# The identity and the causal mask of forgetting attention, from bfloat16 to float32r

## The chip, the cores and the metric

One core of one Trainium2 chip. The metric is the device time of one execution in microseconds (us). Shorter is better.

## The reference, cut to what matters

A decoder trunk of two layers over 256 tokens of width 1024. Layer 0 mixes tokens with forgetting attention (16 heads of 64), layer 1 with chunkwise retention; each is followed by a mixture of 32 SwiGLU experts of which every token takes two. The change lies in the scores of the attention:

```
def query_block(i):
    ...
    s = jnp.einsum('bhqd,bhkd->bhqk', q_b, k).astype(F32) * scale
    s = s + c_b[..., :, None] - cum[..., None, :]
    q_pos = start + jnp.arange(Q_BLOCK)
    s = jnp.where(k_pos[None, :] <= q_pos[:, None], s, NEG_INF)
    p = jax.nn.softmax(s, axis=-1)
    return jnp.einsum('bhqk,bhkd->bhqd', p.astype(v.dtype), v)
```

with Q_BLOCK = 128 and NEG_INF = -1e30. So of 256 keys, queries 0 to 127 see the keys 0 to 127 under a triangular mask, and queries 128 to 255 see the keys 0 to 127 fully and 128 to 255 under the same triangular mask.

## The kernel before

The program runs through four phases in this order: attention (`phase_a`), the experts of layer 0 (`phase_moe`), retention (`phase_c`), the experts of layer 1. All weights, some 460 MB, are streamed from HBM once, through 26 slots of SBUF of 8 KB per partition each. The queue of SP issues every weight transfer (L169) in a fixed order, each as soon as a slot for it is free; a slot comes free when the last instruction that reads it is done. What paces the stream is therefore the DMA engines where slots are free, and the engines that use up the slots where they are not.

In `phase_a` the projections run as steps, one step per block of 128 input channels. A weight block is cut into a high and a low float32r part by ScalarE (L456) and VectorE (L467), up to four blocks ahead, and TensorE makes three kinds of products from the parts (L500 with 256 moving columns, L512 to L514 with 512). A small list, `steps`, says which other work is put between two steps: `steps.at(n, f)` emits f behind step n. Every engine runs its own instructions in the order of the program.

The heads are worked in eight pairs, at steps 25, 29, 33, 38, 46, 49, 52 and 55. `scores` (L713 to L727) fills two PSUM banks, one for each head of a pair: four terms for the queries 128 to 255 against all 256 keys (L721, 256 columns), four for the queries 0 to 127 against the keys 0 to 127 (L724, 128 columns). These use 64 of the 128 rows of the array, one head the upper and one the lower half. Then the mask is added by products of an identity with a triangle of 0 and -1e30 (L726, L727), all 128 rows, 128 columns, two for each bank and so four for each pair, 32 in all. Identity and triangle, `idb` and `cab`, are bfloat16 views of the tile `half`, which comes by one DMA from a table (L600). In the next steps follow the row maximum (L734, L735), the exponential (L741, L742), the division, three transposes for each head (L765) and the products with the values (L778, L779).

`og` is a slot of eight chunks of 256 float32 columns. Chunks 0 to 3 take the output of the first heads, chunk 4 the running sum of the gate's logarithm, chunk 6 and a part of 7 small weights early on. Chunk 5 is first written by `evict_T` behind step 57, which is behind the last scores.

Of the kernel before, what the change touches and what calls it, by code (L numbers as in the profile page):

```python
# [13 lines left out]
F32R = mybir.dt.float32r  # L14
BF16 = mybir.dt.bfloat16
I32 = mybir.dt.int32
AF = mybir.ActivationFunctionType
# [4 lines left out]
P = 128  # L22
# [208 lines left out]
def trunk(ctx, tc, x, fox_w_in, fox_b_f, fox_w_out, ret_w_in, ret_gn_gain, ret_w_out,  # L231
# [3 lines left out]
    mm = nc.tensor.matmul  # L235
    V, A, G, PE = nc.vector, nc.scalar, nc.gpsimd, nc.tensor
# [5 lines left out]
    def bank(tag, dtype=F32):  # L242
        bufs = {"acc": 4, "sc": 2, "pt": 1, "o": 1}[tag]
        return ps.tile([P, 512], dtype, name=tag, tag=tag, bufs=bufs)

    def small(name, n, bufs=1, dtype=F32):
        return cp.tile([P, n], dtype, name=name, tag=name, bufs=bufs)
# [5 lines left out]
    def new_slot(i, dtype, units=1):  # L253

        k = i, units, dtype
        if k not in made:
            made[k] = nc.alloc_sbuf_tensor_at(f"slot_{len(made)}", [P, 2048 * units], dtype,
                                              offset=slot_base + 8192 * i)
        return made[k].ap()
# [70 lines left out]
    ident = small("ident", P)  # L330
# [41 lines left out]
    idb, cab, trb = (half.bitcast(BF16)[:, P * i:P * i + P] for i in range(3))  # L372
# [202 lines left out]
    def phase_a():  # L575
# [11 lines left out]
        ids = {}  # L587

        def chunks(n, dtype=F32):
            ids[n], a = st.claim(dtype)  # L590
            return a.rearrange("p (c q) -> p c q", c=8)


        og = chunks("og")
        cT, wf = og[:, 4, :], og[:, 6, 0:P].rearrange("p (k h) -> p k h", k=8)
        bf = small("bf", 16)
        for n in range(2):
            nc.sync.dma_start(wf[:, 4 * n:4 * n + 4, :], fw[n][:, :, 4096:4112])
# [35 lines left out]
        steps = Steps()  # L634
# [6 lines left out]
        def forget_0():  # L641
            G.tensor_tensor(wf, wf, gT[:, 0, :, None].to_broadcast([P, 8, 16]), ALU.mult)
            wfb = wf[:, :, None, :].to_broadcast([P, 8, 8, 16])
            G.tensor_copy(wfh.rearrange("p k (r h) -> p k r h", r=8), wfb)

        def forget_half():
            pk = small("pk", 16)
            V.tensor_tensor(pk, bf, cst[:, C_E16:C_E16 + 16], ALU.mult)
            V.tensor_reduce(bfp, pk, AX.X, ALU.add)
            G.tensor_tensor(wf, wf, wfh[:, :, 0:16].bitcast(F32), ALU.subtract)  # L650
            A.activation(wfl.rearrange("p k (r h) -> p k r h", r=8), wf[:, :, None, :].to_broadcast([P, 8, 8, 16]),
                         AF.Copy)
# [60 lines left out]
        def scores(hp):  # L713
            bs = [bank("sc"), bank("sc")]
            pr[hp] = bs
            (qh, ql), (kh, kl) = q2[hp // 4], k2[hp // 4]
            c = hp % 4
            terms = ((ql[:, c], kh[:, c]), (qh[:, c], kh[:, c]), (qh[:, c], kl[:, c]), (bq, bias[:, hp % 7]))
            for i, (q, k) in enumerate(terms):
                for b, r in zip(bs, own):  # L720
                    mm(b[:, 128:384], q[r, 128:256], k[r, :], start=i == 0, stop=False, skip_group_check=True)  # L721
            for q, k in terms:
                for b, r in zip(bs, own):
                    mm(b[:, 0:128], q[r, 0:128], k[r, 0:128], start=False, stop=False, skip_group_check=True)  # L724
            for b in bs:
                mm(b[:, 0:128], idb, cab, start=False, stop=True, skip_group_check=True)  # L726
                mm(b[:, 256:384], idb, cab, start=False, stop=True, skip_group_check=True)  # L727

        nms = {}

# [51 lines left out]
        def heads(hp, s):  # L782
            steps.at(s, lambda: scores(hp))
            steps.at(s + 1, lambda: after_scores(hp))
            steps.at(s + 2, lambda: after_first(hp))
            steps.at(s + 3, lambda: norm(hp, 1))
            steps.at(s + 4, lambda: ptrans(hp, 0))
            steps.at(s + 6, lambda: ptrans(hp, 1))
            steps.at(s + 7, lambda: pv(hp))
# [63 lines left out]
        steps.at(5, row_rstd)  # L853
        steps.at(10, rows)
        steps.at(1, forget_0)
        steps.at(6, forget_half)
        for n, f in ((12, forget_1), (14, forget_2), (17, forget_3), (19, forget_4), (20, forget_5)):
            steps.at(n, f)
        steps.at(30, lambda: router_gains(0, raw))
# [12 lines left out]
        for u in range(2):  # L872
            b = [bank("acc"), bank("acc")]
# [9 lines left out]
            b = [bank("acc"), bank("acc")]  # L883
            proj_T(f"Ak{u}", xs, cuts, b, steps)
            evict_qk(u, b, 1, (17, 41)[u], 1.0)
            b = [bank("acc"), bank("acc")]
            proj_tok(f"Av{u}", xk, cuts, b, steps)
            evict_v(u, b)
        for u in range(2):
            b = [bank("acc"), bank("acc")]  # L890
# [647 lines left out]
    def final_norm():  # L1538
# [34 lines left out]
        yield  # L1573

    g = phase_a()
    if STOP == "A":
        done = True
# [35 lines left out]
```

## Time and profile before

| | us |
|---|---|
| median of 3 runs | 1239.19 |
| lowest and highest run | 1238.94 and 1240.21 |
| the profiled execution | 1238.94 |
| its span, from the first to the last instruction | 1237.0 |
| busy: TensorE matmul | 984.1 |
| busy: TensorE weight load (overlaps the matmuls) | 634.2 |
| busy: VectorE | 413.4 |
| busy: ScalarE | 318.5 |

In the profile PE is TensorE's matmuls, PEld its weight loads, DVE VectorE, ACT ScalarE, SP the engine whose queue issues the weight transfers. A row of the timeline gives start, duration, engine, line, operation and operands, and xN says that N instructions of the same kind in a row are merged into it; with a narrow window the merge is cut to those that overlap the window. Matmuls are pipelined, so their durations overlap; the distance from start to start is what one costs in a stream.

### The profile page before, as it was taken

The page shows a single profiled execution, that of the slowest core. Times are in us where ns is not written, and L with a number is a line of the kernel's source. Part 1 is how long each engine was busy: PE and PEld are TensorE (multiplying, and loading weights), DVE is VectorE, ACT ScalarE, POOL GpSimd, SP SyncE. Part 2 cuts the span into 40 slices and gives each one's busy share as a digit, 9 for nine tenths or more (in the row PEclk, how much of TensorE's full clock was granted, in tenths as well). Part 3 has the DMA queues.
Part 4 walks back from the last instruction along what each step waited for, and adds up shares of the span by engine and source line. Part 5 has one row for each costly group of instructions (what it writes and reads, how often), then busy time and mean ns, then how long its engine had stood idle before and what let it go on. Part 6 is the DMA issues. An engine that isn't in the chain of part 4 may idle for free. (4 is left out here: it accounts for less than half of the span.)

```text
span 1237.0 us, 21654 instructions
## 1 busy us (share of the span) xinstructions
PE 984.1 (80%) x9275; PEld 634.2 (51%) x9275; DVE 413.4 (33%) x934; ACT 318.5 (26%) x674; POOL 38.1 (3%) x46
## 2 busy tenths in 40 slices
PE   9999996686776766678999999987677666667776
PEld 8888863343332323244889888744333333233343
DVE  5776732112111111111678676421211111111112
ACT  5665621011010100000555575321110101100102
POOL 1000000000000000000133100000000000000000
PEclk9999999899987979789999999999999787878899
DMA  9965889999999999999992777989999999999996
GB/s 336 338 260 196 322 303 422 419 426 428 425 427 429 427 426 427 426 429 399 371 369 69 251 259 284 362 363 419 423 427 426 428 428 426 429 425 427 428 424 241
DMA packets 74407, 462.18 MB, mean 374 GB/s; under 512 B 8881, under 2 KB 13761, under 8 KB 42050
## 3 DMA queue, kind: packets, MB, share of 16 engines
q1 hardware_dynamic: 73600, 460.14, 91.8%
q8 instruction: 75, 1.23, 0.4%
q10 hardware_dynamic: 706, 0.60, 0.1%
q14 instruction: 26, 0.21, 0.0%
HBM read 459.67 MB, written 1.05 MB: 372 GB/s over the span
## 5 line engine op out<-in xcount | busy, mean ns | idle before, releaser
L1073 PE MATMUL sc<-slot,slot 128*32 128x256 f32 x4096 | 272.2, 417 | 47.5 <-DMA slot<-in_expert_w_gu_dram 42.9
L1073 PEld LDWEIGHTS sc<-slot,slot 128*32 128x32 f32 x4096 | 136.3, 118 | 171.2 <-issue 54.6
L1104 PE MATMUL o<-slot,half 128*32 128x256 f32 x1984 | 137.3, 421 | 97.7 <-DMA slot<-in_expert_w_down_dram 50.0
L1104 PEld LDWEIGHTS o<-slot,half 128*32 128x32 f32 x1984 | 69.6, 118 | 160.3 <-issue 64.1
L1083 DVE TENSOR_TENSOR rB<-rB,sc 128x128 f32<-128x128 f32 x64 | 23.8, 372 | 373.8 <-ACT rB L1082 373.8
L467 DVE SCALAR_TENSOR_TENSOR slot<-slot,gT,slot 128x512 fp32r<-128x512 f32 x160 | 121.8, 781 | 53.0 <-ACT slot L456 51.6
L500 PE MATMUL acc<-slot,slot 128*128 128x256 f32 x960 | 125.6, 288 | 1.7 <-ACT slot L456 1.3
L456 ACT ACTIVATE slot<-slot,gT 128x512 fp32r<-128x512 f32 x159 | 110.9, 719 | 41.1 <-PE acc L514 15.9
L500 PEld LDWEIGHTS acc<-slot,slot 128*128 128x128 f32 x960 | 119.1, 193 | 4.1 <-ACT slot L456 1.7
L1122 DVE COPY slot<-o 32x256 f32<-32x256 f32 x124 | 51.8, 418 | 197.8 <-PE o L1104 170.5
L1120 ACT ACTIVATE slot<-o 32x256 f32<-32x256 f32 x124 | 46.5, 375 | 276.5 <-DVE slot L1122 276.5
L1082 ACT ACTIVATE rB<-sc 128x128 f32<-128x128 f32 x64 | 17.7, 277 | 360.5 <-PE sc L1073 360.5
L512 PE MATMUL acc<-slot,slot 128*128 128x512 f32 x256 | 102.6, 401 | 0.0
L970 PE MATMUL sc<-h,slot 128*128 128x512 f32 x112 | 75.3, 836 | 33.5 <-DVE slot L957 33.5
L513 PE MATMUL acc<-slot,slot 128*128 128x512 f32 x256 | 100.2, 391 | 1.6 <-DVE slot L467 1.6
L514 PE MATMUL acc<-slot,slot 128*128 128x512 f32 x256 | 100.2, 392 | 0.0
L1133 PE MATMUL acc<-slot,slot 128*128 128x512 f32 (+1 forms) x128 | 60.9, 611 | 13.4 <-ACT slot L1120 13.2
L970 PEld LDWEIGHTS sc<-h,slot 128*128 128x128 f32 x112 | 28.8, 269 | 77.3 <-issue 77.3
L513 PEld LDWEIGHTS acc<-slot,slot 128*128 128x128 f32 x256 | 48.3, 189 | 11.4 <-DVE slot L467 2.5
L514 PEld LDWEIGHTS acc<-slot,slot 128*128 128x128 f32 x256 | 48.1, 188 | 10.1
L512 PEld LDWEIGHTS acc<-slot,slot 128*128 128x128 f32 x256 | 48.2, 188 | 9.3 <-issue 0.3
L978 DVE TENSOR_TENSOR slot<-pt,gT 128x512 f32<-128x512 f32 x28 | 19.4, 692 | 99.1 <-PE pt L977 99.1
(243 smaller groups left out, 756.8 us busy)
## 6 DMA issues: line engine op xcount, KB each, us to landing
slot<-in_expert_w_gu_dram SPq DMA_DIRECT2D x84, 2048.0 KB, 39.1
slot<-in_expert_w_gu_dram SPq DMA_DIRECT2D x86, 1024.0 KB, 9.5
slot<-in_expert_w_down_dram SPq DMA_DIRECT2D x42, 2048.0 KB, 39.1
slot<-in_expert_w_down_dram SPq DMA_DIRECT2D x40, 1024.0 KB, 10.7
slot<-in_ret_w_in_dram SPq DMA_DIRECT2D x24, 1024.0 KB, 14.1
slot<-in_fox_w_in_dram SPq DMA_DIRECT2D x15, 1024.0 KB, 11.8
slot<-in_ret_w_out_dram SPq DMA_DIRECT2D x8, 1024.0 KB, 8.2
slot<-in_fox_w_out_dram SPq DMA_DIRECT2D x4, 1024.0 KB, 15.2
```

The source lines that it names most:

```text
L456: A.activation(wh, w, AF.Copy, scale=1.0 if g is None else g)
L467: V.scalar_tensor_tensor(wl, w, g, wh, ALU.mult, ALU.subtract)
L500: mm(o, w[:, P * j:P * j + P], x[:, k, :], start=first and k == 0 and j % 2 == 0, stop=last and k == 7, skip_group_check=True)
L512: mm(banks[t], xh[:, q], wh, start=first and k == ks[0], stop=False)
L513: mm(banks[t], xh[:, q], wl, start=False, stop=False)
L514: mm(banks[t], xl[:, q], wh, start=False, stop=last and k == ks[-1])
L970: mm(b, o[:, t, :], h[:, t, 512 * n:512 * n + 512], start=t == 0, stop=t == 1)
L1073: mm(bgu[32 * j:32 * j + 32, 0:256].rearrange("p (two f) -> p two f", two=2), xg[:, kk, 32 * e4:32 * e4 + 32], wv[:, :, P * j:P * j + P], ...
L1104: mm(by[32 * nb:32 * nb + 32, 0:256], gTt[:, 32 * j:32 * j + 32], w[:, j % n, 256 * nb:256 * nb + 256], start=j == 0, stop=j == 3, skip_gr ...
L1120: A.activation(o, i, AF.Copy)
L1122: V.tensor_copy(o, i)
L1133: mm(sums[t, n], w2["scm"][0:rows, P * t:P * t + P], y4[0:rows, 512 * n:512 * n + 512], start=start, stop=False, skip_group_check=True)
```

## The change

A float32r view of chunk 5 of the slot `og` takes a copy of the identity and of the triangle. Two new ScalarE instructions, put behind step 11, make these copies from the bfloat16 views. The 32 mask products read the copies in place of the bfloat16 views.

```
+        idca = new_slot(ids["og"], F32R).rearrange("p (c q) -> p c q", c=8)[:, 5, :]
+        idr, car = idca[:, 0:P], idca[:, P:]
...
+        def masks():
+            A.activation(idr, ident, AF.Copy)
+            A.activation(car, cab, AF.Copy)
...
             for b in bs:
-                mm(b[:, 0:128], idb, cab, start=False, stop=True, skip_group_check=True)
-                mm(b[:, 256:384], idb, cab, start=False, stop=True, skip_group_check=True)
+                mm(b[:, 0:128], idr, car, start=False, stop=True, skip_group_check=True)
+                mm(b[:, 256:384], idr, car, start=False, stop=True, skip_group_check=True)
...
         steps.at(6, forget_half)
+        steps.at(11, masks)
```

The identity is copied from the float32 tile `ident`, the triangle from `cab`.

## Rows read from the trace of the kernel before

**Rows 1.** The page's second part: the span in 40 slices of 31 us, busy tenths of TensorE, and the mean busy share of the DMA engines.
```profile
PE   9999996686776766678999999987677666667776
...
DMA  9965889999999999999992777989999999999996
```
**Rows 2.** The chain of work that ended last, in order of time: start, duration, what. Its pieces before 918 us are TensorE and its helpers back to 855 us, where the chain begins.
```profile
855.40 3.69 PE sc L1073 x64
...
918.55 39.38 DMA slot<-in_expert_w_down_dram
...
1111.34 39.08 DMA slot<-in_expert_w_down_dram
...
1205.38 17.56 DMA slot<-in_expert_w_down_dram
```
**Rows 3.** Busy time by stretch: us, busy time and instructions of each engine, granted clock, DMA share, GB/s. The end of the attention phase and the first experts.
```profile
160.00:165.00 5.00, 4.50 (x38) 4.29 (x38) 3.42 (x24) 1.30 (x4) 0.69 (x1) 1.00 1.01 380
165.00:170.00 5.00, 4.89 (x49) 2.96 (x53) 1.73 (x7) 1.67 (x2) 0.00 (x0) 1.00 0.16 67
170.00:175.00 5.00, 5.00 (x64) 2.33 (x56) 2.90 (x17) 1.82 (x3) 0.00 (x0) 1.00 0.69 223
...
180.00:185.00 5.00, 3.88 (x67) 2.08 (x65) 2.20 (x6) 1.03 (x3) 0.00 (x0) 1.00 1.00 423
```
**Rows 4.** What the queue of SP waited for between 160 and 175 us: us in total, times, longest.
```profile
SPq L169 <- PE sc L1073: 12.1, 3, 10.6
```
**Rows 5.** Busy time by stretch while the scores are worked, columns as in rows 3.
```profile
60.00:70.00 10.00, 10.00 (x101) 9.17 (x98) 7.51 (x20) 5.49 (x15) 0.00 (x0) 1.00 0.92 350
70.00:80.00 10.00, 10.00 (x94) 9.36 (x94) 7.22 (x19) 6.90 (x17) 0.00 (x0) 1.00 0.31 106
...
100.00:110.00 10.00, 9.34 (x94) 8.70 (x93) 6.60 (x19) 6.72 (x18) 0.00 (x0) 1.00 0.36 120
```
**Rows 6.** What TensorE's matmuls waited for between 50 and 120 us: us in total, times, longest.
```profile
PE acc L513 <- DVE slot L467: 1.6, 1, 1.6
PE sc L721 <- ACT slot L742: 0.7, 1, 0.7
```
**Rows 7.** Groups by line, engine, operation and shape between 0 and 190 us: count, busy us, mean ns of one, idle before.
```profile
L726 PE MATMUL sc<-half 128*128 128x128 bf16 x16 | 2.7, 225 | 0.0
...
L724 PEld LDWEIGHTS sc<-slot,slot 64*128 64x128 f32 x48 | 3.6, 187 | 0.0
...
L727 PEld LDWEIGHTS <-half 128*128 128x128 bf16 x16 | 1.6, 98 | 0.0
```
**Rows 8.** The timeline of TensorE around the first group of mask products, matmuls and then weight loads.
```profile
53.49 0.28 PE L724 MATMUL sc<-slot 64*128 64x128 f32 x2
53.70 0.23 PE L726 MATMUL sc<-half 128*128 128x128 bf16 x1
53.77 0.22 PE L727 MATMUL sc<-half 128*128 128x128 bf16 x1
53.83 0.22 PE L726 MATMUL sc<-half 128*128 128x128 bf16 x1
53.88 0.22 PE L727 MATMUL sc<-half 128*128 128x128 bf16 x1
...
53.70 0.10 PEld L726 LDWEIGHTS <-half 128*128 128x128 bf16 x1
...
53.88 0.19 PEld L500 LDWEIGHTS acc<-slot,slot 128*128 128x128 f32 x1
...
53.99 0.31 PEld L500 LDWEIGHTS acc<-slot,slot 128*128 128x128 f32 x2
```
**Rows 9.** The same view elsewhere, where 32-bit operands follow each other on the array: L724 before its masks, L659 and its neighbours, and L523, which is two products of the program (one for each token half).
```profile
53.32 0.19 PEld L724 LDWEIGHTS sc<-slot,slot 64*128 64x128 f32 x2
53.44 0.19 PEld L724 LDWEIGHTS sc<-slot 64*128 64x128 f32 x2
...
29.33 0.28 PE L659 MATMUL sc<-slot,slot 128*128 128x256 f32 x1
29.45 0.28 PE L660 MATMUL sc<-slot,slot 128*128 128x256 f32 x1
...
25.91 0.71 PE L523 MATMUL pt<-slot,ones 128*128 128x128 f32 x4
26.38 3.12 PE L500 MATMUL acc<-slot,slot 128*128 128x256 f32 x24
```
**Rows 10.** The same view where the used rows of the array change between two products that both read 32-bit operands: from L500 (128 rows) to L721 (64 rows).
```profile
52.43 0.28 PE L500 MATMUL acc<-slot,slot 128*128 128x256 f32 x1
52.64 0.39 PE L721 MATMUL sc<-slot,slot 64*128 64x256 f32 x2
```
**Rows 11.** The timeline of ScalarE around step 11, with the idle time before a row and what ended it in brackets.
```profile
26.66 0.38 ACT L524 ACTIVATE rB<-pt 128x256 f32<-128x256 f32 x1 [1.93 <-PE pt L523]
26.94 1.94 ACT L456 ACTIVATE slot<-slot,gT 128x512 fp32r<-128x512 f32 x3
29.05 0.72 ACT L456 ACTIVATE slot<-slot,gT 128x512 fp32r<-128x512 f32 x1 [0.18 <-PE acc L500]
33.38 0.72 ACT L456 ACTIVATE slot<-slot,gT 128x512 fp32r<-128x512 f32 x1 [3.60 <-PE acc L500]
```
**Rows 12.** Groups of ScalarE on 128 x 128 elements between 0 and 190 us, columns as in rows 7.
```profile
L741 ACT ACTIVATE slot<-sc,nm 128x128 f32<-128x128 f32 x16 | 5.8, 365 | 18.4 <-DVE nm L735 18.4
...
L1082 ACT ACTIVATE rB<-sc 128x128 f32<-128x128 f32 x2 | 0.6, 278 | 2.6 <-PE sc L1073 2.6
```
**Rows 13.** The tile `half` up to 60 us: duration of its DMA's issue and when it was issued; and the time from issue to landing.
```profile
L600 SPq DMA_DIRECT2D half<-cst_dram x1: 635/635/635, 9.4 to 9.4; - x1
...
DMA to landing us min/median/max: 4.9/4.9/4.9
```

## The prediction

> **What bounds the kernel now.** I read the slices first, to find the stages, then the chain of waits, the busy time by stretch, and only then the timeline of TensorE at the changed products. In the slices [rows 1] the reader is to see two kinds of stage. Counted from 0, in the slices 6 to 18 and 27 to 38 the DMA engines are busy throughout and TensorE is not: the experts wait for their weights. In the slices 0 to 5, and again in 19 to 25, it is TensorE that is full, and the DMA has holes (2 to 4, 21 to 24): attention and retention use up the slots more slowly than DMA could fill them. The chain of waits [rows 2] says the same of the end: from 918 us on it is one weight transfer behind another, before that TensorE.
>
> The change lies in a stage of the second kind. While the scores are worked, from 53 to 117 us, TensorE is busy 9.3 to 10 us of every 10 and the DMA share falls to 0.31 [rows 5]; between 50 and 120 us the matmuls waited twice, once for a weight block (L513) and once, 0.7 us, within the scores (L721) [rows 6]. So time added to TensorE there moves all that follows. It reaches the end if nothing absorbs it on the way. The DMA engines' last hole before the experts is at 165 to 175 us (shares of 0.16 and 0.69) and then the share is 1.00 [rows 3]; that hole is SP waiting for a slot that TensorE gives free by the first expert's products [rows 4]. A later TensorE makes the hole longer by the same amount, and from there on the stream has no slack to catch up. In the retention phase, which starts when the last expert of layer 0 has been loaded, the same happens again. I therefore pass a delay of TensorE in this phase on to the end one for one.
>
> **The change part by part.** *The 32 mask products.* Eight groups of four. Before, such a product costs little: in the stream the four start at 53.70, 53.77, 53.83 and 53.88 us, 0.055 us apart [rows 8], and a weight load of bfloat16 shows 98 ns where one of 32-bit operands shows 187 [rows 7]. What a group costs I measure from the first mask's weight load at 53.70 to the second weight load of L500 at 53.99, because a load starts when the product before it enters the array, so 53.99 is when the first product of L500 really begins: 0.29 us [rows 8]. L500's own load is 0.11 of it (53.88 to 53.99).
>
> After, no row shows a float32r product with 128 columns and all 128 rows, so its distance p in a stream has to be bounded. From below: 0.055 us, the present distance, if the format didn't matter. The nearest rows speak for double: L724 has 128 columns of the same format on half the rows, and its pairs of weight loads stand 0.12 us apart (53.32, 53.44); L659 and L660, all rows and 256 columns, 0.12 us [rows 9]; L500's load takes 0.11 before its product begins [rows 8]. L523, 128 columns and all rows in plain float32, has four records in the 0.47 us up to the start of L500 (25.91 to 26.38), 0.12 each [rows 9]. Since 128 and 256 columns give nearly the same distance, it is the weight load that sets it, and I take p = 0.11. From above: 0.165 us, the load of 0.11 with the streaming of 128 columns (0.055, from the bfloat16 rows) behind it in place of beside it.
>
> With the first load at the same 53.70, the four products begin at p, 2p, 3p and 4p after it, L500's load begins with the fourth and takes 0.11: 4p + 0.11. The extra per group is 4p + 0.11 - 0.29 = 4p - 0.18, which is 0.26 us at p = 0.11, and for eight groups **2.1 us**. (At 0.108 it is 2.0, at 0.12 it is 2.4.)
>
> The Trainium skill speaks against this change, in "TensorE: Matmul & The Clock Gate", section "Weight-path perf modes": a fast weight load applies to 128 weights of a type other than FP32, so the mask loses it; here bfloat16 loads show 98 ns and 32-bit ones 187. Its section "LDWEIGHTS" gives columns / 1.2 ns, 107 ns for 128 columns; an estimate of the sum by this page is 8 x (4 x 0.107 - 0.18) = 2.0 us.
>
> *The gap ahead of the masks.* From the last pair of L724 (53.49) to the first mask are 0.21 us in place of 0.11 [rows 8]. This looks like the price of changing formats, which the change would save. But from L500 to L721, both float32r, the gap is 0.21 too (52.43 to 52.64) [rows 10], while from L523 to L500 the format changes and all rows stay, and L500 starts at 26.38 behind a last record at about 26.34 (25.91 + 0.71, less 0.28 for a single one) [rows 9]. What these two gaps share is the change between 64 and 128 rows, and that stays. I book no saving; were it the format, the first load would move up by up to 0.20 us a group.
>
> *The two copies.* ScalarE on 128 x 128 elements takes 278 to 365 ns [rows 12], two of them 0.56 to 0.73 us, once. No row shows a copy from bfloat16 to float32r of this size; a gain is excluded, since ScalarE does nothing less. They stand behind L524 and one cut of a weight block, so in the row of three L456 at 26.94 us. Queued behind them on ScalarE are the cuts for later steps; VectorE's L467 and then TensorE wait for these. The cover: TensorE works on 24 products of the gate from 29.33 us for some 2.9 us before it needs the next cut block, and ScalarE itself idles 3.60 us until 33.38 us because its buffers are not free [rows 9, 11]. So nothing of it reaches TensorE. Without this cover it would be 0.7 us, once.
>
> *Waits and queues.* The copy waits for the tile `half`, issued at 9.4 us and landed 4.9 us later [rows 13], 13 us before. The first mask product now waits for ScalarE's second copy, done by about 28.5 us, 25 us before. No DMA is added or moved, so SP's queue is passed by nothing; GpSimd isn't touched. Chunk 5 of `og` has no other user in between, and its next writer stands behind the scores as before. Each of these costs nothing. The granted clock is 1.00 in this stage [rows 5], its upper level, and TensorE gets no idle time by the change.
>
> *Sum.* 8 x 0.26 = 2.1 us on the span of 1237.0 us of the profiled execution, which took 1238.94 us with what lies around it: 1241.0 us. The median of the runs is 0.25 above that execution: 1241.3 us, 0.17% more. A measurement of this kernel can tell about 0.2%, 2.5 us, from no change.
>
> **The rivals.** *Slower by more: load and stream don't overlap.* At each of the eight groups p is 0.165; the fourth product begins at 0.11 + 3 x 0.165 = 0.605, streams 0.055, and L500 loads 0.11: 0.77 - 0.29 = 0.48 us a group, 3.8 us, 1243.0 us. It decides from 4p - 0.18 = 2.5 / 8, so p above 0.123 us. Against it: L659's distance of 0.12 us is too short for a load of 0.11 and 256 columns one after the other [rows 9], so there they overlap; for it: no row shows it at 128 columns and all rows. The Trainium skill has this rule, in the same page, "The mechanism" of Part 3: loads overlap running matmuls only when the row group differs. The trace of L659 disagrees, as all its products use the same rows.
>
> *Slower: two passes.* L523 is two products of the program and shows four records [rows 9]; plain float32 is split. Were the mask split too, the group has eight loads: 8 x 0.11 + 0.11 - 0.29 = 0.70 us, 5.6 us, 1244.8 us. Against it, L659 in float32r has one record for a product.
>
> *The gap goes with the format.* The first load moves up 0.20 us: the extra is 0.06 a group, 1239.7 us; with p = 0.055 as well it is 4 x 0.055 - 0.18 - 0.20 = -0.16, 1237.9 us. For it: the gap is there; against it: rows 10.
>
> *Hidden.* The pairs of heads are paced by the softmax and not by TensorE, and a longer group only shortens TensorE's wait. For it: the wait of 0.7 us for L742 [rows 6]; against it: one wait in eight pairs, and the softmax itself starts from the masked scores. Then 1239.2 to 1240 us.
>
> **How the numbers follow.** The forecast 0.67, no overlap 0.08, two passes 0.03, the gap 0.12, hidden 0.10. The predicted time is the forecast's, 1241.3 us, with its own range of 1240.4 to 1242.2. The range goes down to 1238.9, which leaves out only the gain end of the gap, and up to 1243.2, which takes in the case of no overlap and leaves out two passes. Slower by over 0.2%: no overlap, two passes, and 0.10 of the forecast (p towards 0.12, and runs that spread over 1.3 us): 0.21. Faster by over 0.2%: hardly any row gives it, 0.03 from the far end of the gap. Within: 0.76.
>
> **What would show it.** After, the mask's weight loads show about 0.19 us in place of 0.10, and the mask products stand 0.11 us apart. The gap of 0.21 ahead of them stays; if it has shrunk to 0.11, the format was its cause. From the first mask's load to L500's second load are 0.55 us. ScalarE has two new rows of about 0.3 us near 28 us, and TensorE doesn't wait longer for L456. The first expert's products and the hole in the DMA share come about 2 us later, as do the last transfers. I am wrong if a group shows 0.55 us and the end doesn't move (then the delay is absorbed, and the waits of L721 have shrunk), if the masks stand 0.16 apart, or if there are eight records in a group.

## The result, and the profile after

The changed kernel takes 1254.07 us (median of 4 runs, 1253.09 to 1255.74) where the kernel before takes 1239.70 beside it: a ratio of 1.0118, with a 95% interval of 1.0106 to 1.0130. That is 14.4 us more, seven times the 2.1 us of the forecast, and outside the range. The profiled execution has a span of 1251.1 us, against 1237.0 before.

The slices, counted from 0 as in the prediction, show at a glance where it happens. TensorE's busy tenths in slice 1 (31 to 62 us) are 5 where they were 9 [rows 1], and the DMA share in slice 2 is 3 where it was 6:

```profile
PE   8599997777675757578999999987777666566676
...
DMA  9936779999999999999992767989999999999996
```

The timeline of ScalarE around step 11, which answers to [rows 11], names the place. L650 and L651 are the two copies, L650 of the identity from the float32 tile `ident` and L651 of the triangle from the bfloat16 view, so that only the second reads `half`; the brackets hold the idle time before a row and what ended it:

```profile
26.37 0.39 ACT L524 ACTIVATE rB<-pt 128x256 f32<-128x256 f32 x1 [1.93 <-PE pt L523]
26.66 0.71 ACT L456 ACTIVATE slot<-slot,gT 128x512 fp32r<-128x512 f32 x1
43.42 0.31 ACT L650 ACTIVATE slot<-ident 128x128 fp32r<-128x128 f32 x1 [16.05 <-DMA slot<-in_router_expert_w_dram]
43.63 0.29 ACT L651 ACTIVATE slot<-half 128x128 fp32r<-128x128 bf16 x1
```

The copies themselves take 0.6 us, as foreseen. But the first of them waits 16 us for a transfer that it doesn't read: the router weights of layer 0, which land in `og` as well, in columns 1664 to 1951 of the slot, while the copies go to columns 1280 to 1535. In the kernel before, this transfer was issued at 37.84 us and landed 5.7 us later, at 43.5 us (SP's timeline, and the view of the transfer):

```profile
37.84 1.31 SPq L357 DMA_DIRECT2D slot<-in_router_expert_w_dram  x1
DMA to landing us min/median/max: 5.7/5.7/5.7
```

Behind the waiting copy are the cuts of the weights (L456). The waits of all engines between 20 and 45 us (us in total, times, longest) show the chain from there:

```profile
DVE slot L467 <- ACT slot L456: 20.5, 3, 16.4
ACT slot L650 <- DMA slot<-in_router_expert_w_dram: 16.0, 1, 16.0
...
PE acc L500 <- ACT slot L456: 12.3, 2, 11.1
```

VectorE and TensorE both wait for ScalarE's cuts. Three rows of TensorE's timeline hold the loss:

```profile
31.92 1.60 PE L500 MATMUL acc<-slot,slot 128*128 128x256 f32 x12
44.59 6.23 PE L500 MATMUL acc<-slot,slot 128*128 128x256 f32 x36 [11.07 <-ACT slot L456]
50.66 0.40 PE L512 MATMUL acc<-slot,slot 128*128 128x512 f32 x1
```

After an idle 11.07 us the next 36 products need 44.59 to 50.66, 6.07 us. The busy time by stretch (columns as in [rows 3]) shows why that is slow: the granted clock, 1.00 up to 36 us, has gone to 0.50, the lower of its two levels (1.2 GHz in place of 2.4), and rises again only in the course of the products, to 0.90 as the mean of 48 to 50 us:

```profile
36.00:40.00 4.00, 0.00 (x0) 0.00 (x0) 0.00 (x0) 0.00 (x0) 0.00 (x0) 0.77 1.05 378
40.00:44.00 4.00, 0.00 (x0) 0.00 (x0) 0.00 (x0) 0.58 (x3) 0.00 (x0) 0.50 0.43 85
44.00:46.00 2.00, 1.41 (x6) 1.41 (x7) 1.43 (x3) 2.00 (x4) 0.81 (x2) 0.50 0.97 274
46.00:48.00 2.00, 2.00 (x12) 2.00 (x11) 2.00 (x5) 1.70 (x4) 0.00 (x0) 0.50 1.05 401
48.00:50.00 2.00, 2.00 (x17) 2.00 (x17) 1.93 (x5) 1.28 (x2) 0.00 (x0) 0.90 1.04 400
```

The mask products are a separate and smaller cost, and here the forecast held. The first group, matmuls and then weight loads, answers to [rows 8]:

```profile
66.06 0.28 PE L731 MATMUL sc<-slot 64*128 64x128 f32 x2
66.27 0.33 PE L733 MATMUL sc<-slot 128*128 128x128 f32 x1
...
66.27 0.19 PEld L733 LDWEIGHTS sc<-slot 128*128 128x128 f32 x1
66.38 0.19 PEld L734 LDWEIGHTS sc<-slot 128*128 128x128 f32 x1
66.48 0.19 PEld L733 LDWEIGHTS sc<-slot 128*128 128x128 f32 x1
66.59 0.19 PEld L734 LDWEIGHTS sc<-slot 128*128 128x128 f32 x1
...
66.71 0.30 PEld L500 LDWEIGHTS acc<-slot,slot 128*128 128x128 f32 x2
```

The loads are 0.11 us apart, and the gap of 0.21 us ahead of the group is still there. The second load of L500 is at 66.71 + 0.30 - 0.19 = 66.82 us, 0.55 us behind the first mask's load, where it was 0.29.

**The sum.** The first products of the scores begin at 65.20 us in place of 52.64, 12.6 us later: the 11.07 us of idle time and about 1.7 us of slow products, less 0.3 us by which this execution was ahead of the other before the stall (L524 at 26.37 in place of 26.66 us). The first product of the experts begins at 184.12 us in place of 169.50, 14.6 us later, of which 8 x 0.26 = 2.1 us are the masks'. From there on the slices run as before, and the span ends 14.1 us later:

```profile
64.88 0.40 PE L500 MATMUL acc<-slot,slot 128*128 128x256 f32 x2
65.20 0.39 PE L728 MATMUL sc<-slot,slot 64*128 64x256 f32 x2
...
184.12 1.07 PE L1081 MATMUL sc<-slot,slot 128*32 128x256 f32 x16
```

For the comparison, the same product of the kernel before:

```profile
169.50 0.85 PE L1073 MATMUL sc<-slot,slot 128*32 128x256 f32 x12
```

### The profile page after: what moved, and what is told of

Same layout as the page of the kernel before. It is cut to its first block, busy times and chain, and to the rows that moved or that the text cites. A ratio compares the mean times of both kernels' runs of the same rounds, so it can differ in the third digit from the quotient of the medians.

```text
span 1251.1 us, 21658 instructions
## 1 busy us (share of the span) xinstructions
PE 980.3 (78%) x9275; PEld 633.3 (51%) x9275; DVE 413.1 (33%) x934; ACT 319.5 (26%) x676; POOL 37.5 (3%) x46
## 5 line engine op out<-in xcount | busy, mean ns | idle before, releaser
L467 DVE SCALAR_TENSOR_TENSOR slot<-slot,gT,slot 128x512 fp32r<-128x512 f32 x160 | 121.8, 781 | 67.9 <-ACT slot L456 66.5
L500 PE MATMUL acc<-slot,slot 128*128 128x256 f32 x960 | 126.8, 288 | 13.9 <-ACT slot L456 12.8
L500 PEld LDWEIGHTS acc<-slot,slot 128*128 128x128 f32 x960 | 119.7, 193 | 17.0 <-ACT slot L456 13.6
L456 ACT ACTIVATE slot<-slot,gT 128x512 fp32r<-128x512 f32 x159 | 110.9, 718 | 37.9 <-PE acc L514 16.3
L512 PE MATMUL acc<-slot,slot 128*128 128x512 f32 x256 | 102.5, 400 | 0.0
L978 PE MATMUL sc<-h,slot 128*128 128x512 f32 x112 | 72.6, 809 | 33.5 <-DVE slot L965 33.5
L512 PEld LDWEIGHTS acc<-slot,slot 128*128 128x128 f32 x256 | 48.1, 188 | 9.4 <-issue 0.3
```

What stands on the lines that cost most here:

```text
L456: A.activation(wh, w, AF.Copy, scale=1.0 if g is None else g)
L467: V.scalar_tensor_tensor(wl, w, g, wh, ALU.mult, ALU.subtract)
L500: mm(o, w[:, P * j:P * j + P], x[:, k, :], start=first and k == 0 and j % 2 == 0, stop=last and k == 7, skip_group_check=True)
L512: mm(banks[t], xh[:, q], wh, start=first and k == ks[0], stop=False)
L978: mm(b, o[:, t, :], h[:, t, 512 * n:512 * n + 512], start=t == 0, stop=t == 1)
```

## The experiments

Theory A: the copy at step 11 is made to wait for the two router transfers because they write another part of the same slot; the cuts queue behind it; that is some 12.5 us, and the mask products are 2.1 us. Rival B: it is the float32r products, or what they wait for. Rival C: there is a wait, but for the table `half` or for a count that other transfers share, not for the router's transfers. The edits are against the changed kernel unless said otherwise. Each time stands beside runs of the kernel before on the same chip (medians of 1239.1 to 1239.8 us).

**The copies alone.**

```
-                mm(b[:, 0:128], idr, car, start=False, stop=True, skip_group_check=True)
-                mm(b[:, 256:384], idr, car, start=False, stop=True, skip_group_check=True)
+                mm(b[:, 0:128], idb, cab, start=False, stop=True, skip_group_check=True)
+                mm(b[:, 256:384], idb, cab, start=False, stop=True, skip_group_check=True)
```

> The two copies at step 11 stay as in the changed kernel, the 32 mask products read the bfloat16 views again. Theory A (the copies wait at step 11 for the two router transfers, which write other columns of the same slot, and the cuts of weights queue behind them): ScalarE stalls 16 us again, TensorE waits some 11 us, time 1239.7 + 12.5 = 1252 us. Rival B (the float32r mask products, or what they wait for, cost the time): no stall matters, about 1240 us.

Measured: 1252.04 us, ratio 1.0108 (1.0091 to 1.0125). The copy waits again, and TensorE with it:

```profile
43.49 0.31 ACT L650 ACTIVATE slot<-ident 128x128 fp32r<-128x128 f32 x1 [16.54 <-DMA slot<-in_router_expert_w_dram]
```

```profile
44.66 6.98 PE L500 MATMUL acc<-slot,slot 128*128 128x256 f32 x36 [11.56 <-ACT slot L456]
```

(the first fence is ScalarE's timeline, the second TensorE's). 12.9 us are there without a single float32r mask product. Rival B is out.

**The copies later.**

```
-        steps.at(11, masks)
+        steps.at(21, masks)
```

> The whole change, but the copies stand behind step 21 in place of 11, when the router transfers have landed and still ahead of the first scores at step 25. Theory A: no stall, only the products' 8 x 0.26 = 2.1 us are left, 1241.8 us. Rival B: the 14 us stay, 1254 us.

Measured: 1241.08 us, ratio 1.0017 (1.0008 to 1.0027): 2.0 us more than before, the products' share. In this kernel the copies still wait, but for something else in the slot, and for so short a time that nothing late comes of it (timeline of ScalarE):

```profile
48.13 0.31 ACT L650 ACTIVATE slot<-ident 128x128 fp32r<-128x128 f32 x1 [2.92 <-DVE slot L699]
```

L699 is the VectorE instruction that reads the running sum from chunk 4 of `og`, again columns that the copy doesn't touch. TensorE's longest wait behind it is 1.6 us for L467, as long as in the kernel before [rows 6].

**The copies in another slot.** The chunks of `bias` become a ring of six, and the copies take the chunk that comes free.

```
-        idca = new_slot(ids["og"], F32R).rearrange("p (c q) -> p c q", c=8)[:, 5, :]
-        idr, car = idca[:, 0:P], idca[:, P:]
+        idr, car = bias[:, 6, 0:P], bias[:, 6, P:]
...
-            ch = bias[:, 6, :]
+            ch = bias[:, 5, :]
...
-        A.activation(bias[:, hp % 7, :], ...
+        A.activation(bias[:, hp % 6, :], ...
...
-        (bq, bias[:, hp % 7])
+        (bq, bias[:, hp % 6])
```

> The whole change with the copies at step 11, but they are written into a chunk of the slot bias (whose ring of seven bias chunks becomes one of six), which no transfer writes. Theory A: the copies wait for nothing but the table, landed by 15 us: no stall, 1241.8 us. Rival C (the copies wait for the transfer of the table itself, or for a count that the transfers on its semaphore share): the stall stays, 1254 us.

Measured: 1241.14 us, ratio 1.0015 (1.0005 to 1.0024). At the same place in ScalarE's queue the copies wait for nothing (timeline of ScalarE):

```profile
26.39 0.71 ACT L456 ACTIVATE slot<-slot,gT 128x512 fp32r<-128x512 f32 x1
27.01 0.30 ACT L649 ACTIVATE slot<-ident 128x128 fp32r<-128x128 f32 x1
27.21 0.30 ACT L650 ACTIVATE slot<-half 128x128 fp32r<-128x128 bf16 x1
27.41 0.71 ACT L456 ACTIVATE slot<-slot,gT 128x512 fp32r<-128x512 f32 x1
```

They read the same table in the same step, so it isn't the table that they waited for. Rival C is out.

**The router weights elsewhere.**

```
-        raw = og[:, 6:8, :].rearrange("p c q -> p (c q)")[:, P:P + 288]
+        raw = vt[:, 1, 512:800]
```

> The whole change as it is, copies at step 11 into chunk 5 of og, but the router weights are loaded into free columns of the slot v in place of og. Theory A: no stall, 1241.8 us. Rival C: the stall stays, 1254 us. If it is the slot og as such and not the router transfers in it that makes the copies wait, the stall stays too.

Measured: 1241.09 us, ratio 1.0018 (1.0008 to 1.0028), and the copies run at 27.03 us. With the transfers out of the slot, the copies may stay in it.

**The same columns under one name.** The products read the bfloat16 views, and the copies are float32, under the name `og`.

```
-            A.activation(idr, ident, AF.Copy)
-            A.activation(car, cab, AF.Copy)
+            A.activation(og[:, 5, 0:P], ident, AF.Copy)
+            A.activation(og[:, 5, P:], cab, AF.Copy)
```

> The mask products read the bfloat16 views. The two copies stand at step 11 and go to the same 256 columns of chunk 5 of og, but as float32 under the name og, under which the router transfers are written too, in place of the float32r view under a name of its own; nothing reads them. If the wait comes from the second name (columns are told apart within one name and not between two): no stall, 1239.2 us. If it comes from the slot, whatever the name: the stall stays, 1252 us as with the copies alone.

Measured: 1239.18 us, ratio 1.0002 (0.9993 to 1.0011), no stall (timeline of ScalarE):

```profile
26.75 0.30 ACT L648 ACTIVATE slot<-ident 128x128 f32<-128x128 f32 x1
26.95 0.30 ACT L649 ACTIVATE slot<-half 128x128 f32<-128x128 bf16 x1
```

Same slot, same columns, same step as with the copies alone, 12.9 us apart in time. What differs is the name and, with it, the type that is written; the type by itself is out, for the float32r copies into the bias slot wait for nothing. So the wait isn't one of the hardware but one that the program carries. The float32r view and `og` are two tensors laid over the same memory, and between them the whole slot counted as touched, while within `og` the columns were told apart. That the waits are derived in this way from the reads and writes of the tensors is read off these runs; no run shows the derivation itself.

**The router transfers ahead of the gains.**

```
-        for i in range(1, 4):
-            load_gain(nc.sync, i)
         raw = og[:, 6:8, :].rearrange("p c q -> p (c q)")[:, P:P + 288]
         load_router(0, raw)
+        for i in range(1, 4):
+            load_gain(nc.sync, i)
```

> The whole change with its stall, and the two router transfers put ahead of the three loads of gains on SP's queue, which take 5.8 us there. If the length of the stall is set by the landing of the router transfers: the copies run 5.8 us earlier, at 37.6 us in place of 43.4, TensorE waits 5.3 us in place of 11.1, and the time is 1254.1 - 5.8 = 1248.3 us, or down to 1246.6 us where the granted clock stays up. If the copies wait for something else in the slot: 1254.1 us.

Measured: 1254.30 us, ratio 1.0114 (1.0097 to 1.0131). The expectation for a stall set by the landing missed by 6 us; taken alone, the time fits the other one, that the copies wait for something else in the slot. The trace settles it. The two transfers were issued earlier (SP's timeline), but the copy ran no earlier (ScalarE's):

```profile
32.17 3.34 SPq L357 DMA_DIRECT2D slot<-in_router_expert_w_dram  x1
```

```profile
43.75 0.31 ACT L650 ACTIVATE slot<-ident 128x128 fp32r<-128x128 f32 x1 [16.13 <-DMA slot<-in_router_expert_w_dram]
```

From issue to landing this transfer now took 11.5 us in place of 5.5, so it landed at 43.7 us, no earlier than before. The ten weight transfers of 1 MB ahead of it keep the DMA engines full until about 41 us (in this run a share of 1.06 from 40 to 41 us, then 0.57 and 0.19 in the next two), and it came out behind them either way.

**The router transfers ahead of that backlog.** `load_router(0, raw)` stands right behind the load of `cst`, before the ten weight transfers.

```
         nc.sync.dma_start(cst, cst_d[:, P + BW:])
+        raw = og[:, 6:8, :].rearrange("p c q -> p (c q)")[:, P:P + 288]
+        load_router(0, raw)
...
-        raw = og[:, 6:8, :].rearrange("p c q -> p (c q)")[:, P:P + 288]
-        load_router(0, raw)
```

> The whole change, copies at step 11 into og, and the router transfers issued ahead of the ten weight transfers of 1 MB each that stood before them (about 10 us in place of 36 us), so that they are not behind that backlog on the DMA engines. If the copies wait for the landing of these two transfers: they have landed by about 20 us, no stall, and the time is that of late, 1241.1 us, plus at most the 3.5 us that their issue delays the weights behind them. If the copies wait for something else: 1254.1 us.

Measured: 1242.82 us, ratio 1.0027 (1.0016 to 1.0039). Issued at 11.20 us, the transfer lands 3.6 us later, and the copies run at 27.72 us without a wait:

```profile
27.11 0.72 ACT L456 ACTIVATE slot<-slot,gT 128x512 fp32r<-128x512 f32 x1
27.72 0.30 ACT L650 ACTIVATE slot<-ident 128x128 fp32r<-128x128 f32 x1
```

So the stall lasts until these transfers land: it stays where their landing stays, and goes where the landing comes early. The kernel is 3.4 us above the kernel before it was measured with, the late copies 2.0 us above theirs; the 1.4 us between lie within what the later issue of the weights (14.38 us in place of 10.60) may cost, and were not taken apart.

**TensorE kept busy during the stall.**

```
         steps.at(11, masks)
+        steps.at(13, lambda: keep_warm(48, "pt"))
```

> The whole change with its stall, and 48 idle products (two passes of 0.11 us each, 10.6 us) behind step 13 on TensorE, so that it is busy while ScalarE waits. If a part of the loss is the lower clock after the stall (36 products in 6.07 us where 4.3 would do): the granted clock stays at 1.00 there, 1.7 us come back, 1252.4 us. If the clock plays no part: 1254.1 us.

Measured: 1253.63 us (1252.74 to 1253.69), ratio 1.0115 (1.0100 to 1.0131). The granted clock stays at 1.00 from 36 to 50 us (busy time by stretch, columns as above, first fence), and the same 36 products begin at 45.38 us and are followed by L512 at 49.79, so they take 4.41 us in place of 6.07:

```profile
40.00:44.00 4.00, 3.99 (x36) 3.79 (x34) 0.00 (x0) 0.00 (x0) 0.00 (x0) 1.00 0.34 77
46.00:48.00 2.00, 2.00 (x19) 2.00 (x19) 2.00 (x4) 1.72 (x4) 0.00 (x0) 1.00 1.04 393
```

```profile
45.38 4.57 PE L500 MATMUL acc<-slot,slot 128*128 128x256 f32 x36 [1.39 <-ACT slot L456]
49.79 0.40 PE L512 MATMUL acc<-slot,slot 128*128 128x512 f32 x1
```

The clock's share at that place is thus 1.66 us. In the time of the kernel it isn't shown: beside the kernel before, this version and the changed kernel are both 14.4 us slower, where 1.7 us between them were expected. In the profiled execution the copy ran 0.8 us later than in the changed kernel, as the router transfer was issued later; L512 was 0.87 us earlier, the first product of the experts 0.50 us (183.62 us), and the span ended 0.7 us later all the same.

**One wide mask product for each bank.** First with float32r copies behind step 21, then in the kernel before with its bfloat16 views (idb, cab).

```
-                mm(b[:, 0:128], idr, car, start=False, stop=True, skip_group_check=True)
-                mm(b[:, 256:384], idr, car, start=False, stop=True, skip_group_check=True)
+                mm(b[:, 0:512].rearrange("p (k q) -> p k q", k=2)[:, :, 0:128], idr,
+                   car[:, None, :].to_broadcast([P, 2, P]), start=False, stop=True, skip_group_check=True)
```

> As late (copies behind step 21), but one product of 256 columns for each bank in place of two of 128, so 16 weight loads in place of 32. If the weight load sets what a mask product costs: 2 x 0.12 + 0.11 - 0.29 = 0.06 us a group more than before, 0.5 us, 1239.6 us. If the streamed columns set it: as late, 2.0 us, 1241.1 us.

Measured: 1238.47 us, ratio 0.9996 (0.9987 to 1.0005). The loads of the first group (weight loads, two masks and then two of L500):

```profile
53.52 0.30 PEld L733 LDWEIGHTS sc<-slot 128*128 128x128 f32 x2
53.75 0.31 PEld L500 LDWEIGHTS acc<-slot,slot 128*128 128x128 f32 x2
```

L500's second load is at 53.75 + 0.31 - 0.19 = 53.87, 0.35 us behind the first mask's, as expected (0.29 + 0.06). Half the loads with as many columns, and the 2.0 us are gone from the time (0.5 us more than before was expected, which lies inside the interval): the weight load is what the float32r masks cost.

> The kernel before, with one bfloat16 product of 256 columns for each bank in place of two of 128. There the columns set the cost (0.055 us for 128) and not the load, so two of 0.107 take the place of four of 0.055: no change, 1239.1 us. If each product had a cost of its own beside its columns, it would be faster by up to 16 x 0.05 = 0.8 us.

Measured: 1237.90 us, ratio 0.9989 (0.9980 to 0.9998), so by this interval a little faster, and not unchanged as expected. The same view:

```profile
53.37 0.11 PEld L726 LDWEIGHTS <-half 128*128 128x128 bf16 x2
53.49 0.30 PEld L500 LDWEIGHTS acc<-slot,slot 128*128 128x128 f32 x2
```

L500's second load is at 53.49 + 0.30 - 0.19 = 53.60, 0.23 us behind the first mask's in place of 0.29: 8 x 0.06 = 0.5 us, inside the interval (0.2 to 2.5 us). The expectation left out that the last mask product streams beside L500's weight load; with 256 columns in it (0.107 us beside a load of 0.11), twice as much is hidden there. That is an account that fits the 0.23 us; no run tests it apart. This is the one version whose interval lies wholly below the kernel before.

## Why the prediction was wrong

The step that failed is "Waits and queues". It said that the copy waits for the tile `half` (which only the second of the two reads), landed 13 us before, that chunk 5 of `og` has no other user in between, and that "each of these costs nothing". All three sentences look at the columns that the copy reads and writes. The wait was for the slot: for the router transfers, which are written under another name for the same memory, and whose landing at 43.5 us the trace of before held as well. Of the 16 us of ScalarE's wait, 11.07 came through to TensorE as idle time. "The two copies" went wrong with it: the cover of 2.9 and 3.6 us hides 0.7 us, and so it would have hidden this step alone, but not a wait of 16 us at the head of ScalarE's queue. Among the rivals there was none with a wait in that queue, which is why the range missed.

Point by point, the rest:

- The mask products: p = 0.11 us was forecast and 0.11 measured; 0.55 us from the first mask's load to L500's second was forecast and measured; 2.1 us were forecast and 2.0 measured in each of three versions without the stall (copies late, in the bias slot, beside moved router weights), with intervals of about 1 us to either side.
- The gap of 0.21 us ahead of the masks stayed, as forecast, with one format on both sides of it: it doesn't belong to the format, and the change from 64 to 128 rows is what is left of the two that the prediction named. The rival "the gap goes with the format" is out, and so are "no overlap" (the loads would stand 0.165 apart) and "two passes" (four records in a group, not eight).
- "I pass a delay of TensorE in this phase on to the end one for one": held, for 2 us and, within 0.5 us, for 14 (14.6 at the first product of the experts, 14.1 at the end of the span). The rival "hidden" is out. The wait of 0.7 us for the softmax is still there after.
- "TensorE gets no idle time by the change": wrong; with the idle time the granted clock fell to 0.50, which cost 1.7 us more at that place.

## What to carry to other kernels

A new instruction on an engine that feeds others is priced by the latest thing it can wait for, not by its duration: list every access to the memory behind its operands that stands earlier in the program, transfers included, under every name that this memory has, and look up in the trace when each of them is done. An unused corner of a buffer, taken under a second name, was not free here while a slow transfer into the same buffer was under way; put the new tile into a buffer without such a transfer, or the instruction behind the transfer. (Under the buffer's own name the corner was free, but there only copies that nothing reads were tried.) And where products of few columns move to a wider format, compare the distance of their weight loads with their streaming: here the load was what the 128 columns paid for, and fewer and wider products took the cost away.

## What the runs showed of the hardware

- A small transfer behind a backlog landed with the backlog. The router's 128 KB took 5.5 us from issue to landing when issued at 37.8 us, 11.5 us when issued at 32.2, and 3.6 us when issued at 11.2, ahead of the weights. Moving its issue forward by 5.6 us won nothing.
- An idle time of 11 us in the middle of dense products cost 1.66 us beyond itself at the next 36 products (6.07 us in place of 4.41), through the granted clock, which was 0.50 while the first of them ran.
- float32r products of 128 columns on all 128 rows start 0.11 us apart, bfloat16 ones 0.055; with 256 columns the float32r ones start 0.12 us apart [rows 9]. A load alone takes 0.11, and 256 columns about as much by the bfloat16 distance, so the load of the next weights overlaps the product before it though both use the same rows.
- A group of two bfloat16 products of 256 columns takes 0.23 us where four of 128 columns take 0.29.
